# Forgetting attention in steps of two heads, memory's transposes in the projections' banks, and copies of the recurrence's levels issued earlier

## The chip, the cores and the metric

The kernel runs on one core of one Trainium2 chip. The metric is device time in microseconds from one launch. Before the change it is 774.33 us, the median of three runs (773.83, 774.33, 774.6). The core has TensorE (matmuls and transposes, results in PSUM), VectorE, ScalarE and GpSimd (called PE, DVE, ACT and POOL in the profile), and queues that issue DMAs (SP for most loads, POOL and ACT for some). All engines run beside each other and wait for each other by semaphores.

## The reference, cut to what matters

One layer of a hybrid encoder over 512 rows of width 1024, in float32:

```
h    = rmsnorm(x)
fox_q, fox_k, fox_v, fox_f, hg_q, hg_f, hg_i, hg_g = split(h @ w_in)
A    = forgetting attention: 8 heads of 64; per head
         F = cumsum(log_sigmoid(fox_f + bias))
         s[t,u] = q_t . k_u / 8 + F[t] - F[u]  for u <= t;  softmax over u;  times v
B    = gated linear recurrence: 4 heads, state 128x128, chunks of 64;
         rmsnorm(B) * silu(hg_g)
x   += concat(A, B) @ w_out
x   += cross attention of rmsnorm(x) to rmsnorm(mem): 256 memory rows, 4 heads of 256
x   += relu(rmsnorm(x) @ w1)^2 @ w2         (hidden width 4096)
out  = rmsnorm(x)
```

## The kernel before

Every float32 product with a weight matrix is made of three matmuls: operands are split into a rounded high part and the rest, and high x high, high x rest and rest x high are summed. ScalarE makes the high part and VectorE the rest, for weights too (`split_of`, L169 to L178). A weight panel of 256 columns has two halves; `load_next` (L198) issues its DMAs on SP and emits the two splits, and `next_panel` (L213) keeps one panel ahead of the one in use, in the order of the list `specs` (L137 to L158).

TensorE's order is the program's order (`manual_schedule`, L322). The other engines' order is made by the planner of the tile framework from its own estimate, with priorities by place in the program; `ahead(n)` (L272) moves an instruction's priority forward. Tiles come from pools with a fixed number of buffers: `t2` has ten (512 columns each), the PSUM pools are `mm` (three banks, for projections), `sc` (two, scores), `tr` (two, transposes) and `pv` (one).

The class `Fill` (L276) holds a queue of generators, each a projection; one step of a generator is three matmuls. `fill.run(c)` runs steps until the credit c is used up: a step with 512 columns costs 0.64, one with 256 columns 0.32. So projections are spread as filler between small pieces of work that wait for other engines.

The stages are: the first projections; the recurrence's seven levels (L689 to L739, m = 1 to 64), each with two copies per pair of heads on ScalarE into a tile `mix` (L702, L703), 64-wide matmuls `lv` (L709), masked copies and the scaling of the running queries and keys by the forget products (L734, L735, L737), then filler; the recurrence's chunks (L826); the forgetting attention (L982); the output projection and the cross attention; the MLP, whose down product is summed in seven combined products; and the final norm.

The forgetting attention goes over 32 units: pair of heads p, row block tb of 128 rows, head j of the pair. A unit has: a bias on POOL (`fox_bias`, L914 on: F[t] - F[u] and the causal mask, from the rows `nF`, which `fox_rows` broadcasts by DMA); two score matmuls into an `sc` bank (L932, L933); on VectorE scores plus bias and the row's maximum (L938), the exponential on ScalarE (L940), the reciprocal (L941) and the scaling (L942); tb + 1 transposes into a `tr` bank (L950); their copy to `pts` (ScalarE for j = 0, L954, VectorE for j = 1, L956); and the value products of both heads (`fox_out`, L958), which write into the two column halves of one bank. The loop, shortened:

```
for n in range(len(units) + LAG):          # LAG = 3
    fox_bias(units[n + 1]); fox_scores(units[n])
    fill.run(A1 + A2)                       # 2.2
    if n >= LAG and units[n - LAG][2] == 1: fox_out(*units[n - LAG][0:2])
    fox_T(units[n - 1])
```

Memory's rows are transposed by `mem_T` (L873) in eight chunks of two transposes, each in a `tr` bank, threaded into the filler between steps of the second pair's projection (`zipped`, L304).

At the end, `last_product` (L1366) makes the last of the seven products for row blocks 2 and 3. A block's sum of squares (`squares`, L1397, VectorE), the power -1/2 (`row_scale`, L1402, POOL) and the scaled output (`scale_out`, L1407: one half on ScalarE, one on VectorE, each with its output DMA) follow its last addition. `finish` (L1419) does this for blocks 0 and 1 as they are complete.

Of the kernel before, what the change touches and what calls it, by code (L numbers as in the profile page):

```python
# [16 lines left out]
P = 128  # L17
S = 512
# [10 lines left out]

ZL, ZN = 1, 2  # L30
H1, H2, B0 = 1.0, 1.6, 3.0
GF = 5
WARM, WARM2 = 7, 4
P1, P2, P3, P4, PW = 20, 20, 20, 10, -20
MT, NF, V0, LAG = 3, 2, 1, 3
F1, F2, F3, F4, B1 = 1.6, 2.7, 1.5, 1.0, 2.0
FL = 2.0
A1, A2 = 1.4, 0.8
X1, X2, X3, X4 = 1.5, 2.0, 1.5, 2.0
# [4 lines left out]
def emit(  # L44
# [85 lines left out]
    def panel(w, n0):  # L130
        return [(slice(0, WT), w[:, n0 : n0 + WT].rearrange("(k p) n -> p k n", p=P))]
# [171 lines left out]

    def zipped(a, b, lead):  # L304

        for n, c in enumerate(a):
            yield c
            if n >= lead and (n - lead) % ZN == 0:
                yield next(b, 0.0)
        yield from b  # L310

    def fill_rest(fl):
# [59 lines left out]
    def norm_rows(t, name):  # L372
# [6 lines left out]
        ve.tensor_scalar(t, t, r, None, op0=ALU.mult)  # L379

    def norm_T(src, g, hi, lo, n, name, cs):

        for c in cs:
            ps = tr(f"{name}t{c}", (n,))
            for tb in range(n // P):
                te.transpose(ps[:, tb * P : (tb + 1) * P], src(tb, c), ident)
            hc, lc = chunk(hi, c, slice(0, n)), chunk(lo, c, slice(0, n))
            ac.activation(hc, ps, AF.Identity, scale=g[:, c : c + 1])
            ve.scalar_tensor_tensor(lc, ps, g[:, c : c + 1], f(hc), op0=ALU.mult, op1=ALU.subtract)

# [295 lines left out]
    def halves(a, m):  # L686
        return a.rearrange("p (b two m) -> p b two m", two=2, m=m)

    for li, m in enumerate(mlev):  # L689
        if li == 3:  # L690
# [7 lines left out]
        for hp in range(2):  # L698
            M_ = Mv[hp]
            mix = t2(f"mix{hp}{m}", F32, (NT, P))  # L700
            mv_ = halves(mix.rearrange("p c t -> p (c t)"), m)
            ac.activation(mv_[:, :, 0, :], halves(kt_(2 * hp), m)[:, :, 0, :], AF.Copy)  # L702
            ac.activation(mv_[:, :, 1, :], halves(qt_(2 * hp + 1), m)[:, :, 1, :], AF.Copy)  # L703
            w = 64 if m == 64 else 32
            ps = sc(f"lv{hp}{m}", (NT, 2, w))
            for c in range(NT):
                for o in range(0, P, 2 * w):
                    rhs = bass.AP(M_.tensor, M_.offset + c * P + o + m, [list(M_.ap[0]), [S - m, 2], [2 * m, w // m], [1, m]])
                    te.matmul(ps[o : o + 2 * w, c].rearrange("p u (b m) -> p u b m", m=m), mix[:, c, o : o + 2 * w], rhs, start=True, stop=True)  # L709
            lvs.append(ps)  # L710
        for hp, ps in enumerate(lvs):
# [57 lines left out]

    fill.until("gg")  # L770
    fill.run(F3)
    for hp in range(2):
# [99 lines left out]

    def mem_T():  # L873
        me_hi.extend(s4([4, M], f"meh{t}", R) for t in range(2))
        me_lo.extend(s4([4, M], f"mel{t}", R) for t in range(2))
        for c in range(KC):
            norm_T(lambda tb, c: mt[tb][:, c * P : (c + 1) * P], g_mem, me_hi, me_lo, M, "mn", (c,))
            yield 0.25

# [33 lines left out]

    units = [(p, tb, j) for p in range(4) for tb in range(NT) for j in range(2)]  # L914
    prob, probT, fpv = {}, {}, {}
# [9 lines left out]

    def fox_scores(u):
        p, tb, j = u
        h, n = 2 * p + j, (tb + 1) * P
        ts_ = slice(tb * P, n)
        kh, kl = fk[p]  # L930
        ps = sc(f"ps{h}{tb}")
        te.matmul(ps[:, 0:n], fq[p][j][:, ts_], kh[:, j, 0:n], start=True, stop=False)  # L932
        te.matmul(ps[:, 0:n], fq[p][j][:, ts_], kl[:, j, 0:n], start=False, stop=True)  # L933
        with ahead(P3):
# [23 lines left out]
    def fox_out(p, tb):  # L958
# [14 lines left out]
        if tb == NT - 1:  # L973
            ac.activation(mx_hi[:, p, :], pv, AF.Copy)
            ve.tensor_tensor(mx_lo[:, p, :], pv, f(mx_hi[:, p, :]), ALU.subtract)

    fill.until("proj0")
    fox_bias(units[0])
    fill.run(B1)
    to_mix(*pending)  # L980
    fill.run(B0)
    for n in range(len(units) + LAG):  # L982
        if n < len(units):
            p, tb, j = units[n]
            if (tb, j) == (0, 0):
                fill.until(f"proj{p}")
                if p == 0:
                    fill.add(zipped(fox_proj(1), mem_T(), ZL), "proj1")
                    for i in range(V0):
                        fill.add(mem_v(i))  # L990
                elif p == 1:
                    fill.add(fox_proj(2), "proj2")
                    fill.add(proj_tm(new_fv(), WT, AF.Identity, "fv"), "fv256")
                elif p == 2:
# [4 lines left out]
                    for i in range(4):  # L999
                        fill.add(mem_k(i))  # L1000
            if (tb, j) == (3, 0) and p < 3:
                fox_rows(p + 1)
            if n == 2:
                fill.until("fv0")
            if n + 1 < len(units):
                fox_bias(units[n + 1])
            fox_scores(units[n])
        fill.run(A1 + A2)
        if n >= LAG and units[n - LAG][2] == 1:
            fox_out(*units[n - LAG][0:2])  # L1010
        if 1 <= n <= len(units):
            fox_T(units[n - 1])

# [352 lines left out]
    def last_product(gs, banks):  # L1366
# [39 lines left out]

    def scale_out(tb, half, o, r):  # L1407
        _, cs0, ag = fin[tb]
        rows, cs = slice(tb * P, (tb + 1) * P), slice(half * S, (half + 1) * S)
        ac.activation(o[:, cs0], ag, AF.Identity, scale=r)  # L1410
        ac.dma_start(out[rows, cs0], o[:, cs0])
        ve.scalar_tensor_tensor(o[:, cs], acc[tb][:, cs], r, gfin[half], op0=ALU.mult, op1=ALU.mult)
        nc.sync.dma_start(out[rows, cs], o[:, cs])


    FINAL = (("2", 0), ("7", 1), ("3", 0))
    fin = {}

    def finish(tb, half):  # L1419
# [11 lines left out]
        o = s4([D], f"fo{tb}")  # L1431
        scale_out(tb, half, o, row_scale(squares(tb, o, cs, fin[tb][0], f"fv{tb}"), f"fr{tb}"))

# [49 lines left out]
    first_adds(NG - 1)  # L1483
    hidden_part(NG - 1, PRODUCTS[0])
    mlp_down((NG - 2, NG - 1))

# [27 lines left out]
```

## Time and profile before

| what | value |
|---|---|
| median of three runs | 774.33 us |
| the profiled execution | 774.73 us |
| its span, first to last instruction | 773.0 us |
| TensorE busy | 762.7 us |
| VectorE busy | 526.7 us |
| ScalarE busy | 366.9 us |
| POOL busy | 196.0 us |
| granted TensorE clock, mean | 0.997 |

The profile is of one execution. Its page gives the busy time of each engine, the busy share in 40 slices of the span, the DMA queues, the chain of work that ended last, and the costliest groups of instructions by line, with their idle time before and what ended it. Further views give the waits of an engine, the instructions in order of time, the chain in order of time and the groups between two times. Matmuls overlap, so the times of two matmuls' starts tell more than their durations. A group's line reads: line, engine, operation, output <- inputs, shapes, count, busy us and mean ns, idle us before it.

### The profile page before, as it was taken

The numbers are of one execution on the slowest core, as the hardware profiler recorded it, in microseconds if no ns is written. First come the engines' busy times: TensorE is split into PE (matmuls) and PEld (weight loads), VectorE is DVE, ScalarE is ACT, GpSimd is POOL, SyncE is SP. The second block draws the span as 40 slices with busy tenths as digits, with TensorE's granted clock in tenths as the row PEclk, the third lists the DMA queues.
The fourth block names the chain that finished last, engine by engine and source line by source line (L and its number), as shares of the span: only waits on it lengthen the run. The fifth ranks groups of instructions, "written<-read, shape, count | busy, mean of one in ns | idle before, by whom it ended". The sixth has DMA issues, their size and how long they took to land.

```text
span 773.0 us, 11243 instructions
## 1 busy us (share of the span) xinstructions
PE 762.7 (99%) x4229; PEld 644.9 (83%) x4229; DVE 526.7 (68%) x851; ACT 366.9 (47%) x616; POOL 196.0 (25%) x263
## 2 busy tenths in 40 slices
PE   9999999999999999999999999999999999999996
PEld 6889878988979988888888888888888888888885
DVE  5747755587587656655548656959586767777796
ACT  5655464676465533244434344435353535342552
POOL 7207432424353024410016520100101010101123
PEclk9999999999999999999999999999999999999998
DMA  7543331232444342322212596575748575758602
GB/s 245 191 131 112 89 83 56 81 111 84 163 138 137 110 164 86 105 75 75 71 55 84 197 275 129 158 170 163 188 138 204 140 180 157 191 137 226 127 1 109
DMA packets 79831, 103.03 MB, mean 133 GB/s; under 512 B 4593, under 2 KB 58394, under 8 KB 79778
## 3 DMA queue, kind: packets, MB, share of 16 engines
q1 hardware_dynamic: 70226, 76.61, 31.1%
q0 software_dynamic: 8960, 24.67, 15.3%
q10 hardware_dynamic: 592, 1.05, 0.4%
q8 instruction: 33, 0.54, 0.3%
q14 instruction: 20, 0.16, 0.1%
HBM read 89.71 MB, written 4.21 MB: 122 GB/s over the span
## 4 chain that ended last, share of the span: by engine, by line
PE 98%; DVE 1%; issue 0%; POOL 0%; POOLq 0%; ACT 0%; DVEq 0%; ACTq 0%
PE u L239 8%; PE u L238 8%; PE u L237 8%; PE U L1354 4%; PE U L1353 4%; PE U L1352 4%; PE xq L237 2%; PE xq L238 2%; PE xw L239 2%; PE xq L239 2%; PE xw L238 2%; PE wo L237 2%; PE wo L239 2%; PE xw L237 2%; PE wo L238 2%; PE Y L1354 2%
## 5 line engine op out<-in xcount | busy, mean ns | idle before, releaser
L176 DVE TENSOR_TENSOR wld<-wq,whd 128x1024 fp32r<-128x1024 f32 x56 | 68.5, 1223 | 24.7 <-ACT whd L172 24.6
L237 PE MATMUL u<-x_hi,whu 128*128 128x512 f32 x192 | 74.7, 389 | 0.0
L238 PE MATMUL u<-x_lo,whu 128*128 128x512 f32 x192 | 74.7, 389 | 0.0
L239 PE MATMUL u<-x_hi,wlu 128*128 128x512 f32 x192 | 74.7, 389 | 0.0
L172 ACT ACTIVATE whd<-wq 128x1024 fp32r<-128x1024 f32 x56 | 58.4, 1052 | 30.5 <-PE u L238 21.6
L172 ACT ACTIVATE whu<-wru 128x1024 fp32r<-128x1024 f32 x24 | 25.3, 1053 | 61.4 <-DMA wru<-in_w_dram 61.4
L1228 POOL DMA_DIRECT2D wq<-in_w_dram x16 | 19.4, 1242 | 131.5 <-DMA wq<-in_w_dram 120.0
L176 DVE TENSOR_TENSOR wlu<-wru,whu 128x1024 fp32r<-128x1024 f32 x24 | 29.3, 1221 | 32.2 <-ACT whu L172 32.2
L1352 PE MATMUL U<-whd,hb 128*128 128x512 f32 x120 | 46.7, 389 | 0.0
L1353 PE MATMUL U<-wld,hb 128*128 128x512 f32 x120 | 46.7, 389 | 0.0
L1354 PE MATMUL U<-whd,hb 128*128 128x512 f32 x120 | 46.7, 389 | 0.0
L1228 POOL DMA_DIRECT2D wq<-wq x16 | 14.1, 878 | 121.5 <-DVE wld L176 94.7
L238 PEld LDWEIGHTS u<-x_lo,whu 128*128 128x128 f32 x192 | 36.0, 188 | 7.5
L237 PEld LDWEIGHTS u<-x_hi,whu 128*128 128x128 f32 x192 | 36.0, 188 | 7.5
L239 PEld LDWEIGHTS u<-x_hi,wlu 128*128 128x128 f32 x192 | 36.0, 188 | 7.4
L923 POOL TENSOR_SCALAR bi<-nF,Ft 128x128 f32<-128x128 f32 (+3 forms) x32 | 22.3, 698 | 42.9 <-PE pt L950 20.2
L1291 ACT ACTIVATE sq<-ur 128x512 f32<-128x512 f32 x32 | 20.0, 625 | 26.8 <-DVE ur L1288 26.8
L1288 DVE SCALAR_TENSOR_TENSOR ur<-u,rbc 128x512 f32<-128x512 f32 x32 | 21.9, 688 | 12.8 <-PE u L239 12.8
L940 ACT ACTIVATE bi<-bi,mx 128x128 f32<-128x128 f32 (+3 forms) x32 | 17.9, 560 | 23.3 <-DVE mx L938 23.1
L1352 PEld LDWEIGHTS U<-whd,hb 128*128 128x128 f32 x120 | 22.5, 188 | 4.7
L1353 PEld LDWEIGHTS U<-wld,hb 128*128 128x128 f32 x120 | 22.5, 188 | 4.7
L1354 PEld LDWEIGHTS U<-whd,hb 128*128 128x128 f32 x120 | 22.5, 188 | 4.6
(955 smaller groups left out, 2369.4 us busy)
## 6 DMA issues: line engine op xcount, KB each, us to landing
wq<-in_w_dram SPq DMA_DIRECT2D x40, 512.0 KB, 3.2
wru<-in_w_dram SPq DMA_DIRECT2D x24, 512.0 KB, 3.9
wq<-in_w_dram POOLq DMA_DIRECT2D x16, 512.0 KB, 8.1
wq<-wq POOLq DMA_DIRECT2D x16, 512.0 KB, 4.6
xTd<-xT POOLq DMA_DIRECT2D x4, 512.0 KB, 3.3
nF<-Fd POOLq DMA_DIRECT2D x8, 256.0 KB, 4.4
hT<-xTd POOLq DMA_DIRECT2D x4, 512.0 KB, 4.3
xt<-in_x_dram SPq DMA_DIRECT2D x3, 512.0 KB
```

The lines of the kernel that those rows point to most:

```text
L172: ac.activation(hi, raw, AF.Copy)
L176: ve.tensor_tensor(lo, raw, f(hi), ALU.subtract)
L237: te.matmul(ps, wh, hi, start=n_ == 0 and not begun, stop=False)
L238: te.matmul(ps, wh, lo, start=False, stop=False)
L239: te.matmul(ps, wl, hi, start=False, stop=k == order[-1])
L923: gp.tensor_scalar(bi[:, 0:n], fF[h][:, 0:n], -1.0, Ft[:, tb, h : h + 1], op0=ALU.mult, op1=ALU.add)
L1228: gp.dma_start(raw.rearrange("p (k n) -> p k n", k=2), src, accum_op=ALU.add)
L1288: ve.scalar_tensor_tensor(u, ps, 0.0, rbc2, op0=ALU.max, op1=ALU.mult)
L1291: ac.activation(sqs[g, j][:, i, :], u, AF.Square)
L1352: te.matmul(ps, hi, whi[:, k, :], start=begin, stop=False, skip_group_check=True)
L1353: te.matmul(ps, hi, wlo[:, k, :], start=False, stop=False, skip_group_check=True)
L1354: te.matmul(ps, lo, whi[:, k, :], start=False, stop=k == 1, skip_group_check=True)
```

## The change

It has these parts.

- The loop of the forgetting attention goes over 16 pairs (p, tb) with both heads in a step. A step emits, at odd n, the value products of the two row blocks before the last one, back to back; then the transposes of the last row block for both heads; then memory's transposes (in steps 1 to 4); then the scores and softmax of both heads; then the biases of the next pair; then filler, with a credit by row block (FX: 4.4, 4.4, 5.4, 5.4 for the first pair of heads, 3.4, 4.0, 4.6, 5.2 after it) in place of 2.2 for each unit.
- Memory's transposes are made four at a time (two chunks) in an `mm` bank, by the loop itself, and no longer in the filler.
- The order of the panels: the second half of the value projection follows the second pair's projection, and memory's first value panel follows the third pair's.
- The copies `mix` of a level are emitted at the end of the level before it, ahead of its filler. The extra credit of 2.0 at level 32 (FL) is dropped.
- A one-element exponential (`act1`) follows the gate projection.
- At the end, block 1's scaling is emitted within the last product, after block 2's addition; the sum of squares of block 2's last half is made on ScalarE and added on POOL; blocks 2 and 3 scale from a copy of the final gain in PSUM (`gfin_ps`, in the `pv` bank).

```diff
-    specs += [pair(0), panel(w_in, 1024), pair(1), *xv[0:V0], pair(2), panel(w_in, 1024 + WT), pair(3), *xv[V0:]]
+    specs += [pair(0), panel(w_in, 1024), pair(1), panel(w_in, 1024 + WT), pair(2), *xv[0:V0], pair(3), *xv[V0:]]
...
+    def mixes(m):
+
+        out_ = []
+        for hp in range(2):
+            mix = t2(f"mix{hp}{m}", F32, (NT, P))
+            mv_ = halves(mix.rearrange("p c t -> p (c t)"), m)
+            ac.activation(mv_[:, :, 0, :], halves(kt_(2 * hp), m)[:, :, 0, :], AF.Copy)
+            ac.activation(mv_[:, :, 1, :], halves(qt_(2 * hp + 1), m)[:, :, 1, :], AF.Copy)
+            out_.append(mix)
+        return out_
+
+    mixed = mixes(mlev[0])
...
-        fill.run(2 * F2 + (FL if li == 5 else 0.0))
+        if m < 64:
+            mixed = mixes(2 * m)
+        fill.run(2 * F2)
...
+    act1 = sm(1, "act1")
+    ac.activation(act1, gg[1][:, 1, S - 1 :], AF.Exp, scale=0.0)
...
+    def mem_T(c0):
+
+        ps = mm(f"mnt{c0}", (2, M))
+        for c in (c0, c0 + 1):
+            for t in range(2):
+                te.transpose(ps[:, c - c0, t * P : (t + 1) * P], mt[t][:, c * P : (c + 1) * P], ident)
+        for c in (c0, c0 + 1):
+            hc, lc = chunk(me_hi, c, slice(0, M)), chunk(me_lo, c, slice(0, M))
+            ac.activation(hc, ps[:, c - c0, :], AF.Identity, scale=g_mem[:, c : c + 1])
+            ve.scalar_tensor_tensor(lc, ps[:, c - c0, :], g_mem[:, c : c + 1], f(hc), op0=ALU.mult, op1=ALU.subtract)
...
+        if n == 2:
+            fill.until("fv0")
+        if n >= 3 and n % 2 == 1:
+            for step in pairs[n - 3 : n - 1]:
+                fox_out(*step)
+        if 1 <= n <= len(pairs):
+            for j in range(2):
+                fox_T((*pairs[n - 1], j))
+        if n == 0:
+            me_hi.extend(s4([4, M], f"meh{t}", R) for t in range(2))
+            me_lo.extend(s4([4, M], f"mel{t}", R) for t in range(2))
+        elif n <= KC // 2:
+            mem_T(2 * n - 2)
+        if n < len(pairs):
+            fox_scores(*pairs[n])
+            if n + 1 < len(pairs):
+                fox_biases(n + 1)
+            if tb == 2 and p < 3:
                 fox_rows(p + 1)
...
+        fill.run(FX[min(n // NT, 1)][n % NT])
...
-            o2, e2 = s4([D], "fo2"), fin[2][0]
-            r2_ = row_scale(squares(2, o2, slice(0, S), e2, "fv2"), "fr2")
-            o3, v = s4([D], "fo3"), fin[3][0]
+            o2, o3, v = s4([D], "fo2"), s4([D], "fo3"), fin[3][0]
+            _, half1, o1, r1_ = deferred
+            scale_a(1, o1, r1_)
+            e2 = sm(1, "fv2")
+            ac.activation(o2[:, 0:S], acc[2][:, 0:S], AF.Square, scale=1.0 / 32.0, accum_out=e2)
+            gp.tensor_tensor(e2, e2, fin[2][0], op=ALU.add)
+            r2_ = row_scale(e2, "fr2")
+            dma_a(1, o1)
+            scale_b(1, half1, o1, r1_, gfin[half1])
...
-            scale_out(2, 0, o2, r2_)
-            scale_out(3, 0, o3, row_scale(v, "fr3"))
+            for tb, o, r in ((2, o2, r2_), (3, o3, row_scale(v, "fr3"))):
+                scale_a(tb, o, r)
+                dma_a(tb, o)
+                scale_b(tb, 0, o, r, gfin_ps)
...
+    gfin_ps = pvt("gfin_ps")
+    ac.activation(gfin_ps, gfin[0], AF.Copy)
     mlp_down((NG - 2, NG - 1))
```

`scale_a` is the scaled half on ScalarE, `dma_a` its output DMA on ScalarE's queue, and `scale_b` the half on VectorE with its output DMA on SP; together they were `scale_out`.

More of the change, by code (lines that the diff above doesn't have):

```diff
@@ L699, in emit @@
             M_ = Mv[hp]
[L700 to L703, printed above, removed]
+            mix = mixed[hp]
             w = 64 if m == 64 else 32
@@ L911, in mem_k @@
         kTl.append(kT[:, 1])
-    units = [(p, tb, j) for p in range(4) for tb in range(NT) for j in range(2)]
+    pairs = [(p, tb) for p in range(4) for tb in range(NT)]
     prob, probT, fpv = {}, {}, {}
@@ L975, in fox_out, with fox_biases @@
             ve.tensor_tensor(mx_lo[:, p, :], pv, f(mx_hi[:, p, :]), ALU.subtract)
+    def fox_biases(n):
+        for j in range(2):
+            fox_bias((*pairs[n], j))
     fill.until("proj0")
-    fox_bias(units[0])
+    fox_biases(0)
     fill.run(B1)
@@ L1431, in finish @@
         o = s4([D], f"fo{tb}")
-        scale_out(tb, half, o, row_scale(squares(tb, o, cs, fin[tb][0], f"fv{tb}"), f"fr{tb}"))
+        r = row_scale(squares(tb, o, cs, fin[tb][0], f"fv{tb}"), f"fr{tb}")
+        if tb == 1:
+            deferred.extend((tb, half, o, r))
+            return
+        scale_a(tb, o, r)
+        dma_a(tb, o)
+        scale_b(tb, half, o, r, gfin[half])
     def mlp_up_group(g):
```

90 lines of the change are left out of this document (33 added, 57 removed).

## The prediction

> **What bounds the kernel now.** I read the page's head, busy time and chain first: is one engine the whole story?
>
> ```profile
> span 773.0 us, 11243 instructions
> PE 762.7 (99%) x4229; PEld 644.9 (83%) x4229; DVE 526.7 (68%) x851; ACT 366.9 (47%) x616; POOL 196.0 (25%) x263
> ...
> PE 98%; DVE 1%; issue 0%; POOL 0%; POOLq 0%; ACT 0%; DVEq 0%; ACTq 0%
> ```
>
> TensorE works 762.7 of 773.0 us and carries 98% of the chain. So time can be won in three ways only: where TensorE waits, where its instructions take longer than their work, and in the 8 us after its last matmul. The second view is TensorE's list of waits:
>
> ```profile
> PE lv L709 <- issue: 1.0, 1, 1.0
> PE mnt L386 <- ACT pts L954: 0.2, 1, 0.2
> ```
>
> Both waits stand at places that the change edits. The change neither adds nor removes a matmul: scores, transposes, value products and memory's 16 transposes stay, in another order. I go part by part.
>
> **Copies of the levels in front.** The timeline around the wait of 1.0 (level 64), with the last input of its copies:
>
> ```profile
> 98.78 0.41 DVE L734 TENSOR_TENSOR sta<-sta,F 128x256 f32<-128x256 f32 x1
> ...
> 107.28 1.28 ACT L608 ACT_TABLE_LOAD   x1
> 108.57 1.26 ACT L608 ACTIVATE gg<-gg,r 128x512 f32<-128x512 f32 x2
> ...
> 111.39 0.60 PE L681 MATMUL pFr<-ident,Ft 128*8 128x128 f32 x4
> 111.59 0.69 ACT L608 ACTIVATE gg<-gg,r 128x512 f32<-128x512 f32 x1 [0.67 <-PE gg L267]
> 112.03 0.68 DVE L683 COPY Fr<-pFr 8x512 f32<-8x512 f32 x1 [3.51 <-PE pFr L681]
> 112.17 0.41 ACT L702 ACTIVATE mix<-sta 128x256 f32<-128x256 f32 x1
> 112.48 0.40 ACT L703 ACTIVATE mix<-sta 128x256 f32<-128x256 f32 x1
> 112.98 2.02 PE L709 MATMUL lv<-mov,mix 128*128 128x128 f32 x16 [1.00 <-issue]
> ```
>
> The row's "issue" is ScalarE: the first two mix copies end at 112.88, level 64 starts at 112.98. Their inputs were final at 99.2, yet they ran at 112.17, behind the gate's four evictions (gg) on ScalarE; in the program the copy of Fr stands ahead of them, which waits for TensorE's pFr and takes a tile of the same pool (t2). The change puts the copies for level 64 behind level 32's updates, ahead of Fr and of that level's filler. I take them to run near 99 to 106 and the wait to go: **-1.0**. The change also takes 2.0 of filler credit away in front of level 64 (three steps of three 512-wide matmuls), which brings level 64 forward and puts those steps behind it: nothing for the sum, as the queue ends there anyway. If the copies stayed late, the earlier level would wait longer, and the end is +2.1 (three times 0.69, from the 0.23 per matmul in the next fence). The A copies of level 64 gain room, since the gate's last steps now run before their transposes. act1 moves the one table load of the softmax, like the 1.28 above, to just after the gate; nothing that TensorE needs at once is behind it: 0, at most 1.28 the other way.
>
> **Both heads in a step.** The chain view, where each entry lasts until the next matmul's end:
>
> ```profile
> 164.97 0.37 PE pv L966 x4
> ...
> 171.33 0.59 PE pv L966 x8
> ...
> 175.00 0.44 PE pt L950 x4
> ...
> 178.42 0.81 PE pv L966 x12
> 179.22 0.59 PE pt L950 x4
> ...
> 185.20 1.02 PE pv L966 x16
> ```
>
> The value products cost 0.37, 0.59, 0.81, 1.02 for 4, 8, 12, 16 matmuls: 0.15 for the group and 0.054 for each. Four transposes take 0.44, but 0.59 directly behind a group: another 0.15. So a group of value products pays 0.30 whatever its size. Before, there are 16 groups (a head pair times a row block, each alone); after, two row blocks are emitted back to back at every odd step: 8 groups. 8 x 0.30 = **-2.4**. It lies on TensorE's own path, with nothing beside it. Its bounds are 0 (if the 0.15s belong to each row block) and -2.4; I take -2.4 because the intercept is per group in four sizes. [...]
>
> Other seams are free: the chain shows transposes at 0.11 each beside scores and filler alike, so fewer and longer filler stretches win nothing more.
>
> **Memory's transposes.** They leave the two tr banks, where the transposes of probabilities live, for the three projection banks. The 0.2 wait above goes, with the step it held in its issue queue: **-0.3**, bounds 0 and -0.3. Each takes a projection bank for two scales on ScalarE and two on VectorE; a projection tile comes only every 16 steps, so I cost it at 0. Its cover is the third bank; without it four waits of about 1 each.
>
> **The new wait: the second head.** Before, a head's probabilities had a whole unit between scores and transposes. After, both heads' softmax must fit into one filler stretch, whose shortest is 6 steps of three matmuls. A matmul of the filler in the chain, prices by form between 150 and 275 us, and the timeline of before's slowest softmax:
>
> ```profile
> 207.22 0.23 PE pq L238
> ...
> L941 DVE RECIPROCAL dn<-dn 128x1 f32<-128x1 f32 x32 | 5.1, 159 | 8.6 <-ACT bi L940 8.5
> ...
> L942 DVE TENSOR_SCALAR bi<-bi,dn 128x256 f32<-128x256 f32 x8 | 3.4, 424 | 0.1
> L938 DVE CUSTOM_DVE_ANT_0 bi<-ps,bi 128x256 f32<-128x256 f32 x8 | 3.4, 423 | 2.1 <-PE ps L933 2.0
> ...
> L940 ACT ACTIVATE bi<-bi,mx 128x256 f32<-128x256 f32 x8 | 4.1, 506 | 2.5 <-DVE mx L938 2.3
> ...
> 167.64 1.22 DVE L176 TENSOR_TENSOR wl12b<-wr12b,wh12b 128x1024 fp32r<-128x1024 f32 x1 [0.17 <-ACT wh12b L172]
> 168.43 0.40 PE L933 MATMUL ps<-kl,q 128*128 128x512 f32 x1
> ...
> 173.09 0.49 DVE L942 TENSOR_SCALAR bi<-bi,dn 128x512 f32<-128x512 f32 x1
> ```
>
> Six steps are 6 x 3 x 0.23 = 4.1 us, the tightest at the second row block of pairs 1 and 2 (credit 4.0, no value products before its transposes). One head of 256 columns needs 0.42 + 0.51 + 0.16 + 0.42 = 1.5, about 1.9 with hand-overs; the second head adds some 0.8 of VectorE behind the first: 2.7. One weight split of 1.22 in its way makes 3.9, still inside. The slowest single head took 173.58 - 168.83 = 4.75 at 512 columns; with a second head 5.7, where the stretches are 5 to 6 us. So a wait happens only now and then: bounds 0 and +1.6 at each of two steps (5.7 - 4.1), I take **+0.3** in all, near the typical row.
>
> **Queues and loads.** SP issues the same panels with two of them exchanged (fv's second panel before memory's first): each still has a panel's use of 5 us or more ahead of it, 0. On POOL the biases of the next pair now stand behind this pair's scores, and the two row broadcasts behind these:
>
> ```profile
> L923 POOL TENSOR_SCALAR bi<-nF,Ft 128x128 f32<-128x128 f32 x6 | 5.1, 856 | 4.0 <-DMA nF<-Fd 3.2 <-PE pv L966 0.7
> ...
> L924 POOL TENSOR_SCALAR_AFFINE_SELECT bi<-bi 128x128 f32<-128x128 f32 x28 | 10.9, 391 | 2.1
> ...
> L791 POOL DMA_DIRECT2D nF<-Fd x8: 541/568/660, 140.8 to 224.0; - x8
> ...
> DMA to landing us min/median/max: 3.7/4.4/6.3
> ```
>
> Two biases are 2 x (0.86 + 0.39) = 2.5 us and have a step of over 4: 0 on the path.
>
> **The end.** The timeline after TensorE, and the groups of the power and of the last matmuls:
>
> ```profile
> L1404 POOL TENSOR_TENSOR fr<-fv,mhalf x4: 538/563/986, 760.0 to 766.7; 128x1 f32<-128x1 f32 x4
> ...
> L1379 PE MATMUL Z<-whd,hb x16: 278/283/283, 762.2 to 765.0; 128*128 128x256 f32 x16
> ...
> 764.12 0.75 DVE L1399 CUSTOM_DVE_ANT_0 fo<-acc,fe 128x512 f32<-128x512 f32 x1
> ...
> 765.66 0.42 DVE L1392 TENSOR_TENSOR acc<-Z,acc 128x256 f32<-128x256 f32 x1
> 766.12 0.48 DVE L1399 CUSTOM_DVE_ANT_0 fo<-acc,fv 128x256 f32<-128x256 f32 x1
> ...
> 766.53 0.75 DVE L1412 SCALAR_TENSOR_TENSOR fo<-acc,fr,gfin 128x512 f32<-128x512 f32 x1
> 766.69 0.99 POOL L1404 TENSOR_TENSOR fr<-fv,mhalf 128x1 f32<-128x1 f32 x1 [1.19 <-DVE fv L1399]
> 767.71 0.72 ACT L1410 ACTIVATE fo<-fa,fr 128x512 f32<-128x512 f32 x1 [1.46 <-POOL fr L1404]
> ```
>
> TensorE ends at 765.3, but the last add starts at 765.66, since VectorE is still behind with block 2's squares (0.75). These move to ScalarE, so the add waits for TensorE alone: -0.36. The last power takes 0.99 where the others take 0.54 to 0.57; only it runs beside a scaling whose two large inputs lie in SBUF. The change scales from a PSUM copy (gfin_ps): 0.99 becomes 0.56, -0.43. Then ScalarE's 0.72 is the last step, as before. Sum **-0.8**, bounds -0.36 (the power stays) and -0.8. [...] Block 2's new path (square on ScalarE, add and power on POOL) has until 766.2 and starts near 763.1. The deferred scaling of block 1 fits into VectorE's wait for the last product. The copy gfin_ps lies on ScalarE, 47% busy, 0; uncovered, one copy, some 0.6.
>
> **Sum.** -1.0 - 2.4 - 0.3 + 0.3 - 0.8 = -4.2. The profiled execution: span 773.0, run 774.73, hence 768.8 and 770.5. It lies 0.4 above the median of the runs, 774.33, so I predict 770.1 for the median.
>
> **Rivals.** First, *the second head is late everywhere*: VectorE executes in order, and an unlucky order of splits and evictions holds the second head. From 0.28 on each of 15 steps (4.2 / 15) the whole gain is gone; half of that gives 772.2, all of it 774.3. For it: VectorE's 68%, the 4.75 above. Against: the 2.7 to 3.9 against 4.1. Chance 0.13. [...]
>
> Second, *level 64 still waits*: a wait in place of the one removed. The copies remain behind the gate's evictions on ScalarE and 2.1 of cover is gone: 770.1 + 1.0 + 2.1 = 773.2. Against: inputs ready at 99.2. Chance 0.06.
>
> Third, *merging does not do what it seems to*: the 0.30 is per row block, so 772.5. Chance 0.06.
>
> Fourth, *slower*: the biases. At the third row block (three times) the next pair's broadcasts need buffers of t2, which the value products of the next step free. From there 4.4 to 6.3 for the landing, about 1.1 for issuing, 2.5 for two biases, 2.7 for the softmax: 10.7 to 12.6. By my order TensorE has about 14 us of work until the transposes (two fillers of 5.0 and 4.1, the rest transposes, scores and value products). If POOL is held 3 us more, each change of pair waits 2 us: +6, 776. It decides from 5.8 / 3 = 1.9 at each. Chance 0.07.
>
> **Numbers.** Forecast 0.66 (its own range 768.6 to 771.5: the terms at -5 to -3); all terms at their best with no new wait, 768.5 or below, 0.02. 0.2% of 774.33, 1.5 us, is about what a measurement tells from no change. Faster (below 772.8): 0.66 + 0.02 + 0.06 + half of the first rival, 0.80. Same: its other half and the second rival, 0.13. Slower: 0.07. The range 768.6 to 773.0 leaves out the second and fourth rivals and the worse half of the first.
>
> **What would show it.** Level 64 gone from TensorE's waits, its copies before 107. Eight groups of value products, of 12 and 28, at 0.81 and about 1.68. No wait of TensorE on VectorE's probabilities above 0.5 in sum; several are the first rival, and waits ended by POOL's biases the fourth. The last power at about 0.56, and 6.9 instead of 7.7 us from the last matmul to the span's end. A filler that runs slower beside denser VectorE work would make me wrong without any wait.

## The result and the profile after

| | before | after |
|---|---|---|
| median of the runs, us | 774.47 (773.83 to 774.62) | 769.19 (769.09 to 769.35) |
| profiled execution: run, span, us | 774.73, 773.0 | 769.28, 767.5 |
| VectorE, ScalarE, POOL busy, us | 526.7, 366.9, 196.0 | 523.7, 368.7, 190.5 |

The ratio after to before is 0.9934, with a 95% interval from 0.9922 to 0.9947. The change made the kernel 5.3 us faster. The forecast was 770.1, 4.2 us below.

The page's row of busy time, and TensorE's list of waits, of the kernel after. The columns of the waits are: in total, times, longest.

```profile
PE 759.0 (99%) x4229; PEld 646.0 (84%) x4229; DVE 523.7 (68%) x849; ACT 368.7 (48%) x620; POOL 190.5 (25%) x264
...
PE pst L832 <- DVE rec L853: 0.2, 1, 0.2
```

TensorE works 99% of the span, and the page still puts 98% of the chain on it. The waits at level 64 (1.0) and at memory's transposes (0.2) have gone, the probabilities make no wait, and one wait is new: the recurrence's product pst waits for rec. (A wait of 1.3 us at the warming matmuls is the same in both.)

To see where the time went I cut both traces at four places that both have: the first matmul of pF, the first transpose pa, the first scores ps, and the first matmul wo of the attention's output. The view of windows gives a row for each stretch: its ends and its length, and then the busy time of PE, PEld, DVE, ACT and POOL. Before:

```profile
101.54:116.92 15.38, 14.38 (x102) 11.98 (x101) 7.95 (x20) 10.90 (x19) 5.31 (x11) 1.00 0.26 70
116.92:150.18 33.26, 33.26 (x249) 31.24 (x248) 18.95 (x42) 18.70 (x56) 13.66 (x27) 1.00 0.21 64
150.18:275.47 125.29, 125.10 (x901) 109.12 (x900) 90.11 (x209) 74.58 (x151) 38.22 (x68) 1.00 0.41 130
```

After:

```profile
100.96:115.11 14.15, 14.15 (x103) 11.99 (x102) 9.26 (x21) 8.67 (x12) 5.30 (x11) 1.00 0.28 75
115.11:148.73 33.62, 33.41 (x249) 31.25 (x248) 18.53 (x42) 21.02 (x62) 13.08 (x27) 1.00 0.22 64
148.73:270.79 122.06, 122.06 (x901) 110.42 (x900) 87.46 (x210) 73.37 (x150) 32.95 (x68) 1.00 0.42 134
```

The stretch of level 64 lost 1.23 us, the recurrence gained 0.36, the forgetting attention lost 3.23. The last matmul ended at 765.27 and now at 760.63; from there to the end of the span it was 7.70 us and is 6.89, 0.81 less. The work between wo and there takes 0.04 more. That makes 4.87. The other 0.58 of the span arise earlier: the first cut lies at 101.54 and 100.96, and the first level's first matmul, as far apart, at 65.70 and 65.12. The timeline shows where, in before and in after:

```profile
5.64 1.85 PE L462 MATMUL warm<-zero 128*128 128x512 bf16 x4
```

```profile
5.64 1.20 PE L443 MATMUL warm<-zero 128*128 128x512 bf16 x4
```

The four warming matmuls start some 0.43 us apart in one (1.85 us in all), and in the other 0.39 and then some 0.21 (1.20 us in all). In the other kernels below, whose code up to there is that of one of these two but for the place of the copies in one, the same cut falls between 100.55 and 101.52 (an execution that was slow throughout left out). So this part is the chance of one execution and no gain of the change. The granted clock in the profile reads 1.00 there in both, and no row shows the cause.

The medians differ by 5.28 us, 0.4 more than the 4.87 of the parts; the scatter of single executions hides where that belongs.

### The profile page after: what moved, and what is told of

Its sections match the earlier page's. It is cut to its first block, busy times and chain, and to the rows that moved or that the text cites. A ratio compares the mean times of both kernels' runs of the same rounds, so it can differ in the third digit from the quotient of the medians.

```text
span 767.5 us, 11244 instructions
## 1 busy us (share of the span) xinstructions
PE 759.0 (99%) x4229; PEld 646.0 (84%) x4229; DVE 523.7 (68%) x849; ACT 368.7 (48%) x620; POOL 190.5 (25%) x264
## 4 chain that ended last, share of the span: by engine, by line
PE 98%; DVE 1%; ACT 1%; POOL 0%; issue 0%; DVEq 0%; ACTq 0%
PE u L238 8%; PE u L236 8%; PE u L237 8%; PE U L1371 4%; PE U L1369 4%; PE U L1370 4%; PE xq L236 2%; PE xq L237 2%; PE xw L236 2%; PE xq L238 2%; PE xw L237 2%; PE xw L238 2%; PE wo L236 2%; PE Y L1371 2%; PE wo L238 2%; PE Y L1370 2%
## 5 line engine op out<-in xcount | busy, mean ns | idle before, releaser
L921 POOL TENSOR_SCALAR bi<-nF,Ft 128x128 f32<-128x128 f32 (+3 forms) x32 | 20.6, 654 | 54.6 <-PE pt L953 34.5
L1070 ACT ACTIVATE x_hi<-hT,gv 128x512 fp32r<-128x512 f32 x16 | 11.5, 719 | 28.5 <-DVE hT L1069 28.4
```

What stands on the lines that cost most here:

```text
L921: gp.tensor_scalar(bi[:, 0:n], fF[h][:, 0:n], -1.0, Ft[:, tb, h : h + 1], op0=ALU.mult, op1=ALU.add)
```

## The experiments

The medians of two runs can be told apart by about 1 us. The stretches are steadier: where no edit touches it, the recurrence took 33.59 to 33.64 us in nine executions, the attention 122.06 in four of five kernels and 122.11 in the other. So the verdicts go by the stretches, and the medians are given beside them.

**One row block of value products at a time.**

```diff
-        if n >= 3 and n % 2 == 1:
-            for step in pairs[n - 3 : n - 1]:
-                fox_out(*step)
+        if n >= 2:
+            fox_out(*pairs[n - 2])
```

> The value products go back to one row block at a time, 16 groups in place of 8; steps of both heads stay. Theory (0.30 us for each group whatever its size): the stretch from the first scores to the first projection of attention's output goes from 122.06 to about 124.5 us, value products in sum 9.9 to 11.2 us, the time 771.6 us. Rival (the overhead belongs to each row block, and the gain of the change in this stretch, 3.2 us, came from the merged steps alone): 122.1 us and 769.2 us.

The median is 771.54 us (ratio to before 0.9966, 0.9954 to 0.9978). The stretch and the chain of this kernel, an entry lasting until the next matmul's end:

```profile
148.32:272.68 124.36, 124.36 (x902) 110.02 (x900) 87.54 (x210) 73.14 (x150) 33.77 (x68) 1.00 0.43 131
```

```profile
176.99 0.81 PE pv L969 x12
177.80 1.02 PE pt L953 x8
```

The chain of the kernel after, with a group of two row blocks of 12 matmuls in all, the same eight transposes, and a group of 28:

```profile
168.01 0.81 PE pv L969 x12
...
177.09 0.87 PE pt L953 x8
...
182.99 1.68 PE pv L969 x28
```

Eight groups more cost 2.30 us, 0.29 for each: the price of 0.30 is one for the group and not for the row block. About half of it stands in the pv rows (0.15 + 12 x 0.054 = 0.81, 0.15 + 28 x 0.054 = 1.68); where no group stands ahead, eight transposes take 0.87 in place of 1.02.

**Steps of single heads.**

```diff
+        half = FX[min(n // NT, 1)][n % NT] / 2
         if 1 <= n <= len(pairs):
-            for j in range(2):
-                fox_T((*pairs[n - 1], j))
+            fox_T((*pairs[n - 1], 0))
...
-            fox_scores(*pairs[n])
+            fox_scores(*pairs[n], 0)
+        fill.run(half)
+        if 1 <= n <= len(pairs):
+            fox_T((*pairs[n - 1], 1))
+        if n < len(pairs):
+            fox_scores(*pairs[n], 1)
...
-        fill.run(FX[min(n // NT, 1)][n % NT])
+        fill.run(half)
```

> Each step of two heads is cut in two: transposes and scores of one head, half of the filler, transposes and scores of the other, the other half; the value products stay merged in 8 groups. Theory: the filler's first six to nine matmuls of 512 columns after an interruption take 231 to 236 ns in place of 227, some 0.04 us for each stretch, so 16 more stretches cost 0.5 to 0.8 us: the stretch from the first scores to the first projection of attention's output is 122.6 to 122.9 us and the time 769.7 to 770.0. Rival (the prediction's own: seams other than those of value products are free): 122.1 us and 769.2 us.

```profile
148.74:270.91 122.17, 122.17 (x901) 110.03 (x900) 89.79 (x209) 73.58 (x150) 36.70 (x69) 1.00 0.42 133
```

The median is 769.59 (0.9939, 0.9926 to 0.9953), the stretch 0.11 longer. My theory falls: sixteen more stretches of filler cost 0.11 us in all. The prediction's sentence that seams other than those of value products are free was right. Putting both heads in a step is in itself worth no more than these 0.11 us.

**Memory's transposes: the bank, and the place.**

```diff
-        ps = mm(f"mnt{c0}", (2, M))
+        ps = tr(f"mnt{c0}", (2, M))
```

> Memory's transposes stay beside the attention's own, but go back from the projections' banks to the two banks of the transposed probabilities. Theory one, the prediction's (their 0.3 is a wait for a bank and the step it held up): the stretch from the first scores to the first projection of attention's output grows from 122.06 to 122.3 us or more, with waits of the mnt transposes on the copies pts; the time is 769.5 us. Theory two (the gain of memory's transposes lies in their place behind other transposes, not in the bank): 122.1 us, 769.2 us.

The median is 771.21 (0.996, 0.9945 to 0.9974). Stretch and wait:

```profile
149.00:273.05 124.05, 122.97 (x901) 110.37 (x900) 87.36 (x209) 73.33 (x150) 33.10 (x68) 1.00 0.42 131
...
PE mnt L872 <- ACT pts L957: 1.1, 4, 0.3
```

The bank is worth 2.0 us, far more than either theory had. The list has 1.1 of it, but it counts only TensorE's idle time, and the four places lose 1.7 from start to start: at the first, memory's transposes start 0.64 behind those of the probabilities (154.60 and 155.24), and 0.22 in the kernel after (154.33 and 154.55). With both heads in a step two tiles of probabilities are under way in the two banks, and a third transposed tile came too soon at each of the four steps. In the second run they go back into the filler, where mem_T now passes on the steps of the projection, with two transposes in a tr bank behind every second one:

```diff
-                    fill.add(fox_proj(1), "proj1")
+                    fill.add(mem_T(fox_proj(1)), "proj1")
...
-        elif n <= KC // 2:
-            mem_T(2 * n - 2)
```

> Memory's transposes go back into the filler, a pair of transposes behind every second step of the projection of pair 1, in the banks of the transposed probabilities, as before the change; everything else stays. Of the 3.2 us that the stretch from the first scores to the first projection of attention's output lost, merging the value products explains 2.3 and merged steps 0.1, so 0.8 to 0.9 is left. Theory: it is this move (in the trace of before, the filler's matmul behind each of the 8 pairs of transposes takes 0.32 in place of 0.23 us, and two waits of 0.2 to 0.3 stand beside them): the stretch is 122.7 to 123.0 us, the time 769.8 to 770.1. Rival (the prediction's size, 0.3, and the rest lies in the order of the panels): 122.3 us, 769.5 us.

```profile
148.59:272.38 123.79, 122.94 (x901) 109.85 (x900) 87.35 (x210) 73.66 (x150) 33.20 (x68) 1.00 0.42 132
...
PE pt L955 <- DVE mel L877: 0.8, 2, 0.5
```

The median is 771.3 (0.9962, 0.9949 to 0.9974), the stretch 1.73 longer. Missed: in place of 0.7 to 0.9 from the seams came waits of another kind: now the attention's own transposes wait for a bank that memory's holds until VectorE has scaled it. From start to start these late transposes lose 1.4 of the 1.73 us (the first comes 0.90 behind the filler's matmul ahead of it, at 154.68 and 153.78, where 0.23 is usual). Both runs point to the bank; for the place alone at most some 0.3 is left.

**That part alone, on the kernel before.** The same function in the projections' banks, called behind the transposes of the first four heads.

```diff
-                    fill.add(zipped(fox_proj(1), mem_T(), ZL), "proj1")
+                    fill.add(fox_proj(1), "proj1")
...
             fox_T(units[n - 1])
...
+        elif n <= KC // 2:
+            mem_T(2 * n - 2)
```

> The kernel before with one part of the change alone: memory's transposes stand behind the transposes of the first four heads' probabilities and use the projections' banks; steps of one head, 16 groups of value products, old levels and old end stay. Theory (after the other parts were undone one by one, 3.23 - 2.29 - 0.11 = 0.83 us of the attention stretch is left for this part: 8 filler matmuls of 0.32 in place of 0.23 us, and waits of 0.2 to 0.3 for the two shared banks): the stretch from the first scores to the first projection of attention's output goes from 125.29 to 124.3 to 124.7 us, and the time is 773.4 to 773.8 us. Rival (the prediction's 0.3, the remainder belongs to the new order of the panels): 125.0 us and 774.1 us.

The median is 778.2, slower than before (1.0059, 1.0041 to 1.0076). The stretch, and the waits that are new:

```profile
149.62:278.15 128.53, 125.80 (x901) 109.75 (x900) 90.64 (x209) 74.81 (x151) 38.42 (x68) 1.00 0.41 127
...
PE xv L250 <- ACT meh L881: 1.4, 2, 1.0
...
PE xv L252 <- DVE mel L882: 1.0, 2, 0.9
```

Missed, and for a reason that teaches: before the change the first panel of memory's values (xv) follows pair 1's projection in the filler, and it reads meh and mel, which are now made later. The change puts fv's second panel between them. I had costed that exchange at nothing; without it, the move of memory's transposes loses 3.2 us. The timeline of this run gives an estimate of what the part alone is worth if nothing waits for it: from start to start the xv matmuls that wait lose some 3.4 us and one transpose of probabilities, which waits for a copy of memory's values, 0.5; as the stretch is only 3.2 longer, the move itself gains some 0.7.

**The copies of the levels in their old place.** Made at the level's start, as before; the credit of 2.0 stays away.

```diff
-            mix = mixed[hp]
+            mix = mixes_one(m, hp)
...
-        if m < 64:
-            mixed = mixes(2 * m)
```

> The mix copies of every level are made at the level's start again, as before the change; the filler credit of 2.0 in front of level 64 stays away. Theory (the copies for level 64 stand on ScalarE behind the gate's evictions, and 2.0 of credit less covers them): TensorE waits about 3 us at level 64, the first transpose pa comes about 3.1 us later, and the time is 772.3 us. Rival (the wait was not the copies' place but the credit hid it before; or the evictions come earlier too): a wait of 0 to 1.0 us, 769.2 to 770.2 us.

The median is 770.12 (0.9947, 0.9934 to 0.9961). The stretch, the wait and the timeline at level 64:

```profile
100.57:115.55 14.98, 14.38 (x102) 11.98 (x101) 8.24 (x20) 9.87 (x16) 5.37 (x11) 1.00 0.27 72
...
PE lv L694 <- issue: 0.6, 1, 0.6
...
107.60 1.27 ACT L589 ACTIVATE gg<-gg,r 128x512 f32<-128x512 f32 x2
...
108.75 0.41 ACT L673 ACTIVATE mix<-sta 128x256 f32<-128x256 f32 x1
109.01 0.68 DVE L664 COPY Fr<-pFr 8x512 f32<-8x512 f32 x1 [1.47 <-PE pFr L662]
```

In the kernel after, the first of the same copies:

```profile
97.65 0.42 ACT L676 ACTIVATE mix<-sta 128x256 f32<-128x256 f32 x1 [3.57 <-DVE sta L725]
```

The place of the copies is worth 0.83 us, not 3.1. In the run with the old place they start right behind two of the gate's evictions and ahead of the copy of Fr, so ScalarE's queue held them and not the tile of Fr. Only two evictions stand ahead, since without the credit the other two belong to matmuls behind level 64. So the remaining 0.40 of the 1.23 us come with the credit that went away; that is a difference, not measured by itself.

**Without act1.**

```diff
-    act1 = sm(1, "act1")
-    ac.activation(act1, gg[1][:, 1, S - 1 :], AF.Exp, scale=0.0)
```

> The small exponential act1 is left out; the numbers are unchanged. In the changed kernel the stretch from the first transpose pa to the first scores is 33.62 us, before the change it was 33.26. Theory: the 0.36 us is the table load of 1.28 us that act1 puts on ScalarE right before the recurrence; it pushes the recurrence's first normalisation into the way of memory's row norm on VectorE. Without act1 the stretch is 33.2 to 33.4 us, the load comes back at about 148 us in front of the first softmax, TensorE does not wait for it (some 4.4 us of filler cover it), and the time is 768.9 us. Rival A: the 0.36 comes from the steps of filler that moved behind level 64; then the stretch stays 33.6 and the time 769.2. Rival B: the load in front of the first softmax holds the first transposes of probabilities; then the stretch from the first scores to the first projection of attention's output grows by up to 1.3 us and the time is 769.2 to 770.2.

The recurrence and the attention of this run:

```profile
114.77:148.04 33.27, 33.27 (x249) 31.21 (x248) 18.29 (x40) 18.72 (x56) 12.15 (x26) 1.00 0.23 65
148.04:270.15 122.11, 122.11 (x901) 110.45 (x900) 87.35 (x210) 74.60 (x151) 33.60 (x68) 1.00 0.43 134
```

The 0.35 us of the recurrence come back, the wait of pst is gone from the list, and the load in front of the first softmax costs 0.05. The median, 769.14 (0.9936, 0.9922 to 0.9949), can't tell so little. The way it went shows in the timeline of the kernel after:

```profile
114.92 1.28 ACT L764 ACT_TABLE_LOAD   x1
...
116.80 0.62 ACT L367 ACTIVATE m0j<-mt 128x512 f32<-128x512 f32 x1
...
119.78 0.75 DVE L370 TENSOR_SCALAR mt<-mt,m0r 128x1024 f32<-128x1024 f32 x1 [0.98 <-POOL m0r L360]
...
120.56 0.69 DVE L740 SCALAR_TENSOR_TENSOR qs<-pq,rbc 128x512 f32<-128x512 f32 x1
```

And in the run without act1, where mt is scaled at 114.83 and qs starts as soon as TensorE is done with pq:

```profile
119.76 0.69 DVE L740 SCALAR_TENSOR_TENSOR qs<-pq,rbc 128x512 f32<-128x512 f32 x1 [3.04 <-PE pq L238]
```

With act1 the load delays the squares of memory's rows, these the scaling of mt, and that stands on VectorE just when qs could start; qs, the copies q, kt and the squares hj of the recurrence follow one another, up to rec.

**The end: the gain in SBUF, and the squares on VectorE.**

```diff
-                scale_b(tb, 0, o, r, gfin_ps)
+                scale_b(tb, 0, o, r, gfin[0])
```

> The last two scalings on VectorE take the gain from SBUF again and not from its copy in PSUM. Theory (a VectorE instruction with two large SBUF inputs holds up the power on POOL that runs beside it): the last power takes 0.95 to 1.0 us in place of 0.54, and from the last matmul to the end of the span it is 7.3 us in place of 6.9; the time is 769.6 us. Rival (the 0.99 before was a single late case): 0.54 to 0.57 and 6.9 us, 769.2 us.

The median is 769.62 (0.9939, 0.9924 to 0.9954). The timeline's last rows of this kernel, and then of the kernel after:

```profile
761.45 0.75 DVE L1445 SCALAR_TENSOR_TENSOR fo<-acc,fr,gfin 128x512 f32<-128x512 f32 x1
761.61 0.99 POOL L1429 TENSOR_TENSOR fr<-fv,mhalf 128x1 f32<-128x1 f32 x1 [1.12 <-DVE fv L1424]
762.63 0.72 ACT L1437 ACTIVATE fo<-fa,fr 128x512 f32<-128x512 f32 x1 [1.39 <-POOL fr L1429]
```

```profile
757.79 0.69 DVE L1335 TENSOR_TENSOR acc<-U,acc 128x512 f32<-128x512 f32 x1 [0.36 <-PE U L1396]
...
760.66 0.42 DVE L1415 TENSOR_TENSOR acc<-Z,acc 128x256 f32<-128x256 f32 x1 [0.48 <-PE Z L1396]
...
761.53 1.49 DVE L1445 SCALAR_TENSOR_TENSOR fo<-acc,fr,gfin_ps 128x512 f32<-128x512 f32 x2
761.70 0.54 POOL L1429 TENSOR_TENSOR fr<-fv,mhalf 128x1 f32<-128x1 f32 x1 [1.12 <-DVE fv L1424]
762.27 0.72 ACT L1437 ACTIVATE fo<-fa,fr 128x512 f32<-128x512 f32 x1 [0.94 <-POOL fr L1429]
```

The power takes 0.99 beside the scaling from SBUF and 0.54 beside that from PSUM. From the last matmul's end (760.54 and 760.63) to the start of ScalarE's last scaling it is 2.09 and 1.64: 0.45 us, and to the end of the span 7.34 and 6.89. The scaling itself is no shorter with PSUM (1.49 for two). How the scaling from SBUF makes the power longer, no row shows.

```diff
-            ac.activation(o2[:, 0:S], acc[2][:, 0:S], AF.Square, scale=1.0 / 32.0, accum_out=e2)
-            gp.tensor_tensor(e2, e2, fin[2][0], op=ALU.add)
+            e2 = squares(2, o2, slice(0, S), fin[2][0], "fv2")
```

> The sum of squares of row block 2 goes back from ScalarE to VectorE; the deferred scaling of block 1 and the gain in PSUM stay. Theory (VectorE's 0.75 us of squares and 0.75 us of scaling then both stand in front of the two additions of Z): the last addition starts 0.3 to 0.5 us after it could, and from the last matmul to the end of the span it is 7.2 to 7.4 us in place of 6.9; the time is 769.5 to 769.7 us. Rival (the scaling fits into VectorE's wait either way): 6.9 us.

```profile
758.09 0.69 DVE L1335 TENSOR_TENSOR acc<-U,acc 128x512 f32<-128x512 f32 x1 [0.37 <-PE U L1396]
...
759.49 0.75 DVE L1443 SCALAR_TENSOR_TENSOR fo<-acc,fr,gfin 128x512 f32<-128x512 f32 x1
759.65 0.99 POOL L1427 TENSOR_TENSOR fr<-fv,mhalf 128x1 f32<-128x1 f32 x1 [1.30 <-DVE fv L1422]
...
761.02 0.42 DVE L1413 TENSOR_TENSOR acc<-Z,acc 128x256 f32<-128x256 f32 x1
```

Missed: the median is 769.66 (0.9938, 0.9924 to 0.9953), but the last addition starts 0.10 behind the last matmul's end (760.92), where it is 0.03 in the kernel after, and from there to the end of the span it is 6.96 us, not 7.2 to 7.4. With both jobs VectorE is done just in time. The sum of block U starts as soon as its matmuls are through here too (758.09, waiting for TensorE), since block 1's scaling, which waits for a power, no longer stands ahead of it; before the change that sum starts at 763.40, right behind this scaling. There U's last matmul ends at 762.40 (762.01 + 0.39), and VectorE is idle for 0.67 us in front of the scaling, yet it takes the two in their order:

```profile
762.01 0.39 PE L1379 MATMUL U<-whd,hb 128*128 128x512 f32 x1
...
762.73 0.75 DVE L1412 SCALAR_TENSOR_TENSOR fo<-acc,fr,gfin 128x512 f32<-128x512 f32 x1 [0.67 <-POOL fr L1404]
...
763.40 0.68 DVE L1318 TENSOR_TENSOR acc<-U,acc 128x512 f32<-128x512 f32 x1
```

So the deferral alone brings all but 0.07 of the 0.36 us that I gave to the squares. Whether the squares on ScalarE alone would do it too, no run shows. A second scaling from SBUF beside a power gives 0.99 again.

**How near the second head is.** The first of two kernels cut all of the steps' filler to 60 per cent.

```diff
-FX = (4.4, 4.4, 5.4, 5.4), (3.4, 4.0, 4.6, 5.2)
+FX = (2.64, 2.64, 3.24, 3.24), (2.04, 2.4, 2.76, 3.12)
```

> The filler of each attention step is cut to 60 per cent (credits of 2.0 to 3.2 in place of 3.4 to 5.4); what is left of it runs behind the loop. It measures how far the second head was from being late. Theory (in the changed kernel the probabilities are done 0.97 to 5.0 us before their transposes; the stretches shrink by 1.4 to 2.2 us; five steps would go below zero, by 0.25 to 0.87 us, 2.9 in sum, less what VectorE gains as fewer weight splits fall into a step): the stretch from the first scores to the first projection of attention's output grows by 1 to 3 us, with waits of the transposes on VectorE's last scaling; the time is 770.2 to 772.2 us. Rival (the second head is close to late at every step, the prediction's first rival): waits at ten or more steps, over 5 us, 774 us or more.

Missed: three executions took 783.38 us in the median, 781.52 at the best, beyond both forecasts. In a fourth, the profiled one (1552.3 us), TensorE was slow throughout (busy 1538.5 us, against 759.0 in the kernel after), so its times can't be compared, but its waits show a fault of the experiment: less filler in the steps leaves the next pair's projection to be done at once in front of its scores, which then wait for the keys (four waits of ps for kh, 3.2 us in sum at that pace). The second kernel leaves each pair its filler and only shifts it to the first step:

```diff
-FX = (4.4, 4.4, 5.4, 5.4), (3.4, 4.0, 4.6, 5.2)
+FX = (10.48, 2.64, 3.24, 3.24), (8.92, 2.4, 2.76, 3.12)
```

> The filler of the second to fourth row block's step of each pair is cut to 60 per cent (credits 2.4 to 3.2), and what is cut stands in the first row block's step, so that each pair has the same filler in all and the next pair's projection ends where it did. Theory (in the changed kernel the probabilities of these steps are done 0.97 to 5 us before their transposes; the stretches shrink by 1.4 to 2.2 us; five steps fall below zero by 0.25 to 0.87 us, 2.9 in sum): waits of TensorE on the probabilities at about five steps, the stretch from the first scores to the first projection of attention's output is 123 to 125 us and the time 770.2 to 772.2 us. Rival (the second head is close to late everywhere, the prediction's first rival): waits at nearly all twelve steps and over 5 us. Rival the other way (VectorE's load moves away with the filler, and the latency falls with it): no waits, 122.1 us, 769.2 us.

```profile
149.24:277.17 127.93, 123.78 (x901) 110.70 (x900) 88.82 (x210) 72.49 (x150) 34.74 (x68) 1.00 0.41 128
...
PE pt L953 <- DVE bi L945: 3.5, 4, 1.7
...
PE pv L969 <- DVE pts L959: 0.7, 2, 0.4
```

The median is 775.03 (1.0011, 1.0001 to 1.002): the whole gain and more is gone, 5.87 us in the stretch, twice what I had worked out. The transposes wait for the last scaling of the probabilities, and the value products for the copies behind them, which my sum didn't have. They stand at six places, not at nearly all twelve steps, and from start to start these lose some 5.3 us, where the list has 4.2. So a late second head costs as much as the prediction's first rival had it, but only beyond the credits of this change: it begins between 60 and 100 per cent of them.

**One group for a pair, without act1.** The transposed probabilities of three row blocks get two tiles of 4 KB of their own; the other tiles of that pool are taken in another order, so that none waits for them.

```diff
-        if n >= 3 and n % 2 == 1:
-            for step in pairs[n - 3 : n - 1]:
+        if n >= 5 and n % 4 == 1:
+            for step in pairs[n - 5 : n - 1]:
                 fox_out(*step)
...
-            probT[u] = t2(f"pts{h}{tb}")
+            if tb < 3:
+                probT[u] = ppt[j][:, OFF[tb] : OFF[tb] + n]
+            else:
+                probT[u] = t2(f"pts{h}{tb}")
```

> The changed kernel without act1, and with the value products of all four row blocks of a pair in one group of 40 matmuls, so 4 groups in place of 8; the transposed probabilities of the first three row blocks are kept in two tiles of 4 KB. Theory (0.29 us for each group whatever its size, measured between 16 and 8 groups, and 0.35 for act1): the stretch from the first scores to the first projection of attention's output goes from 122.06 to 120.9 us, groups of 40 take 2.3 us, and the time is 769.2 - 1.15 - 0.35 = 767.7 us. Rival A (the group of 12 no longer stands in front of the third row block's transposes, where 0.97 us were left at the least): waits of up to 1 us at a few steps take it back, 768 to 769 us. Rival B (the overhead comes with the row block's length and not with the group): 122.1 us and 768.9 us.

```profile
148.94:269.75 120.81, 120.81 (x901) 110.55 (x900) 87.57 (x209) 73.53 (x151) 33.58 (x77) 1.00 0.42 134
...
182.23 2.33 PE pv L974 x40
```

The median is 768.02 us (0.992, 0.9905 to 0.9934), the best of all: 1.2 below the changed kernel. The attention is 1.30 shorter than in the run without act1, where 4 x 0.29 = 1.16 was expected, and a group of 40 takes 0.15 + 40 x 0.054 = 2.31. No step waits.

## Why the prediction was right, and where not

- **Value products, -2.4:** right. 16 against 8 groups is 2.30 us, and four groups continue the line. The 0.30 is a price of the group; what in the group costs it, no run shows.
- **Other seams free:** right, nearly; single heads cost 0.11.
- **Copies in front, -1.0:** the mechanism was right, the size 1.23. The copies' place is 0.83 of it, the other 0.40 is a difference that I put down to the filler credit, which I had costed at nothing. "If the copies stayed late, the end is +2.1" was wrong: the run has them late, and 0.83 is lost. I had the credit bring level 64 forward but left all four evictions in front of it.
- **Memory's transposes, -0.3:** mis-sized. By the steps above 3.23 - 2.30 - 0.11 leaves 0.8, and the estimate from the run of that part alone is 0.7. In the trace of before two of their pairs came late behind scores. The first, with the row of an undisturbed pair of scores of this size in after (the second has 0.31 where 0.17 is usual):

```profile
155.81 0.28 PE L933 MATMUL ps<-kl,q 128*128 128x256 f32 x1
156.28 0.44 PE L386 MATMUL mnt<-ident,mt 128*128 128x128 f32 x2 [0.19 <-ACT pts L954]
```

```profile
155.34 0.28 PE L931 MATMUL ps<-kl,q 128*128 128x256 f32 x1
155.46 0.40 PE L236 MATMUL pq<-hn_hi,wh10b 128*128 128x512 f32 x1
```

  From start to start 0.47 where it should be 0.12: 0.35 lost at a wait listed as 0.19. The two places give 0.5. The rest is not placed. What the step missed more is what the move protects: with both heads in a step, the old banks would have cost 2.0.
- **Queues and loads, 0:** right as the change has it, but the exchange of the two panels is a condition, not a detail: without it memory's values come too early for the moved transposes.
- **act1, 0, at most 1.28 the other way:** +0.35, inside the bounds. "Nothing that TensorE needs at once is behind it" was the failing sentence: memory's squares were, and three engines later the recurrence.
- **The new wait of the second head, +0.3:** it did not come. The shifted filler shows that the margin is real and not large.
- **The end, -0.8:** 0.81. The power's 0.43 is shown (0.45 by the run). The 0.36 was put on the wrong edit: the deferral of block 1's scaling alone brings all but 0.07 of it.
- **The sum:** -4.2 against -4.87 between the two traces without the 0.58 of the warming matmuls. The misses are -0.5 for memory, -0.3 for the wait that did not come, -0.2 for level 64 and +0.35 for act1; the rest cancels. That the total is only 0.7 off is in part luck, as act1's loss hides a third of what was missed on the other side.

Of the rivals, the second (level 64 waits) and the third (0.30 per row block) are refuted by the runs. The first and the fourth did not occur: no wait of TensorE is ended by VectorE's probabilities or POOL's biases. How near the fourth is, no run tests; in the trace after, every bias is done at least 3.1 us before the scores that it is added to.

## What to carry to other kernels

When one engine is the whole chain, fit its instruction groups to price = fixed part + number x step, and look for the groups whose fixed part comes back: here 0.29 us for each group of value products, and 0.11 us in all for sixteen more seams of scores and transposes. Before merging steps, count the tiles that are then under way in each pool: two banks were enough for one head at a time, and a third tenant cost 2 us with two. Waits that a profile lists can be less than what they cost: here, from one matmul's start to the next, 0.35 where 0.19 was listed (before) and 0.42 where 0.26 was (memory's transposes in the old banks). And of an operation moved "out of the way", follow what is queued behind it on its own engine to the second and third engine.

## What the runs showed of the hardware

- A whole execution with a slow TensorE: in the profiled run with the filler at 60 per cent the matmuls took far longer than elsewhere, though the granted clock was given as 1.0. The row of one group there and in the kernel after, the columns behind the bar being busy time and mean ns of one:

```profile
L238 PE MATMUL u<-x_hi,wlu 128*128 128x512 f32 x192 | 129.6, 675 | 0.0
```

```profile
L238 PE MATMUL u<-x_hi,wlu 128*128 128x512 f32 x192 | 74.7, 389 | 0.0
```

  Its span was 1550.3 us, against 779.6 to 783.4 in the other three executions of the same kernel. Why, no run shows.
- Beside a VectorE scaling with two large inputs in SBUF the power of 128 numbers takes 0.99 us on POOL in three of three cases (one each in before, with the gain in SBUF, and with the squares on VectorE), else 0.54 to 0.73.
